# Layer A's output projection: where the transposed rows of the first two output units are read, and where the second unit is transposed

## The chip, the cores and the metric

The kernel runs on one core of a Trainium2 chip. The metric is the device time of one execution in microseconds (us). Engines are named as the profile names them: PE multiplies matrices, PEld loads its weights, DVE and ACT are the two engines for elementwise work, POOL here mostly issues small transfers, and SP issues the large ones. Each engine works through its own queue in order; semaphores join the queues.

## The reference: what is computed

Two layers act on a sequence of 256 rows and 2048 columns in f32. Layer A projects the normalised input to q, k, v and a gate, runs a chunked attention, multiplies by the gate and projects back from 4096 to 2048 columns, plus the residual. Layer B does the same with shared keys and values and a forget gate. What concerns the change is the last line of layer A and the first ones of layer B:

```python
x = x + (o * jax.nn.silu(g)) @ a_w_out[layer]
...
h_kv = rms_norm(x, kv_norm)
k_s, v_s = jnp.split(h_kv @ kv_w, 2, axis=-1)
...
h = rms_norm(x, b_norm[lb])
q, g = jnp.split(h @ b_w_in[lb], 2, axis=-1)
```

## The kernel before, in words

**Split operands.** An f32 product is made of three matmuls. Each operand is split into a rounded part `hi` (written by ACT) and the remainder `lo` (written by DVE from the raw value and `hi`); the products hi·hi, lo·hi and hi·lo are summed. Weights come in blocks of 128 x 1024 values (512 KB), loaded by SP into one of six `raw` buffers (`RAW = 6`, tag "raw"), split into one of four pairs of `hi` and `lo` buffers (`SPLIT = 4`), and consumed by PE. So a split can start only when PE is done with the split four places earlier, and a load only when the split that read the buffer is done.

**Feed.** `Feed` holds the whole list of weight blocks. `get` hands PE the next split pair; ahead of that, `fill` keeps four pairs (`DEPTH = 3` and the one handed out) prepared, and `refill` issues loads. `Feed.behind(dst, n)` writes a few elements of `dst` with an ACT instruction that reads the `hi` of the n-th prepared pair: later writers of `dst` then stand behind that split on ACT.

**Layer A's output projection** (`project`, with `ao_order`) makes four units `ao0` to `ao3` of 512 columns each. An entry of the order is a sub-block: a normal one (12 matmuls, one weight block of one unit) or a quad (`Quad.step`: 21 matmuls that do one block of each of two units, from four splits `quad_hi0` to `quad_hi3` of the two raw blocks and of differences of them; the two raw blocks are `one` and `two`). The second half of the order is four normal sub-blocks of `ao2` (its blocks 5 to 8), then quad 0, three normal ones (`ao2` blocks 9 to 11), quad 1, three normal ones, and so on to quad 4, with six normal sub-blocks of `ao3` at the end. In `Quad.split`, `t[:, :, 1]` (line 289) needs only the raw block `two`, `t[:, :, 0]` (line 288) both.

**Turned rows.** When a unit closes (`ao_closed`), its residual sum `xin` is complete (line 760). Layer B needs it transposed, as `x1T`, split again in hi and lo. For units 0 to 2 this is `x1_to_T`: `turn` transposes within 32 x 32 squares on DVE (line 487, into the one buffer `xinY`), 16 small transfers issued by POOL move the squares (line 490, into the one buffer `xinZ`), and four generator steps then read `xinZ`, each with two ACT copies (`x1Th`, line 150) and two DVE subtractions (`x1Tl`, line 151). The list that `ao_closed` returns, `[8, 1, 1, 1]`, says after how many further sub-blocks each of the four reading steps is issued. Unit 3 goes another way (`x_to_T`). The transposition of unit 1 writes the `xinY` that unit 0's 16 transfers read, and unit 1's transfers write the `xinZ` that unit 0's reading steps read.

**Loads of the residual.** `load_xin` (line 744) puts the input's columns of a unit on SP's queue, among the weight loads. The buffer `xin3` reuses storage that the transposition of `xin1` reads.

The order of instructions on each engine is set by the order of issue in this code and by a scheduler that may move an instruction ahead of others that do not depend on it.

Of the kernel before, what the change touches and what calls it, by code (L numbers as in the profile page):

```python
# [12 lines left out]
AF = mybir.ActivationFunctionType  # L13
# [3 lines left out]
P = 128  # L17
S = 256
NT = S // P
# [20 lines left out]
SQ = 32  # L40
# [25 lines left out]
def r32(ap):  # L66
    return ap.bitcast(F32)
# [8 lines left out]
def trunk(ctx, tc, x, x_t, gains, a_w_in, a_rel, a_w_out, kv_w, f_w, f_b, b_w_in, b_w_out, final_norm, out):  # L76
    nc = tc.nc
    pe, act, dve, pool, sp = nc.tensor, nc.scalar, nc.vector, nc.gpsimd, nc.sync
# [13 lines left out]
    def big_tile(shape, dt, name):  # L92
        return big.tile(shape, dt, name=name, tag="big")
# [54 lines left out]
    def split_x1(src, k, like=lambda v: v):  # L148
        hi, lo = like(x1T.h(k)), like(x1T.l(k))
        act.activation(hi, src, AF.Copy)  # L150
        dve.tensor_sub(lo, src, r32(hi))
# [10 lines left out]
    def x_to_T(src, k0):  # L162

        banks = []
        for c in range(0, 4, 2):
            ps = bank(f"xT_{k0 + c}")
            for i in range(2):
                for t in range(NT):
                    pe.transpose(ps[:, i * S + t * P:i * S + (t + 1) * P],
                                 src[t][:, (c + i) * P:(c + i + 1) * P], ident)  # L170
            banks.append(ps)
        for c in range(4):
            split_x1(banks[c // 2][:, c % 2 * S:(c % 2 + 1) * S], k0 + c)
            yield
# [13 lines left out]
    class Feed:  # L188
# [31 lines left out]
        def prepare(self, ahead=True, parts=(slice(None),)):  # L220
            if not self.loaded:
                self.begin()
            if not self.loaded:
                return
            spec, b, raw, (before, behind) = self.loaded.pop(0)
            if not spec:
                self.ready.append(b[0].split(b[1]))
                self.refill()
                return
            if before:  # L230
                before()
            nm, h = spec["name"], b - (spec["nk"] // KB - spec["late"])
            if 0 <= h < spec["kept"]:
                both = big_tile([P, 2, IL, KB, HN], F32R, f"{nm}_keep{b}")
                hi, lo = both[:, 0], both[:, 1]
            else:
                hi = stream.tile([P, IL, KB, HN], F32R, name=f"{nm}_hi{b}", tag="hi", bufs=SPLIT)
                lo = stream.tile([P, IL, KB, HN], F32R, name=f"{nm}_lo{b}", tag="lo", bufs=SPLIT)
            if spec["g0"] is not None:
                for j in range(KB):  # L240
                    gk = gain[:, spec["g0"] + b * KB + j:][:, :1]
                    act.activation(hi[:, :, j], raw[:, :, j], AF.Copy, scale=gk)  # L242
                    dve.scalar_tensor_tensor(lo[:, :, j], raw[:, :, j], gk, r32(hi[:, :, j]),  # L243
                                             op0=OP.mult, op1=OP.subtract)
                parts = ()
            for j in parts:
                act.activation(hi[:, :, j], raw[:, :, j], AF.Copy)  # L247
                dve.tensor_sub(lo[:, :, j], raw[:, :, j], r32(hi[:, :, j]))  # L248
            if behind:
                behind()  # L250
            self.ready.append((hi, lo))
            if ahead:
                self.refill()
# [8 lines left out]
        def behind(self, dst, n):  # L262

            act.activation(dst, r32(self.ready[n][0][:, :, 0, :1]), AF.Copy)
# [12 lines left out]
    class Quad:  # L277
# [4 lines left out]
        def split(self, i):  # L282

            one, two = self.raw
            t = self.all.t[:, 0]
            if not i:
                feed.behind(t[:, :, 0, :1], -1)
                dve.tensor_sub(t[:, :, 0], two[:, :, 0], one[:, :, 0])
                dve.tensor_sub(t[:, :, 1], two[:, :, 1], two[:, :, 0])
            src = [one, t, two[:, :, 1:], one][i]  # L290
            n = src.shape[2]
            hi = stream.tile([P, IL, KB, HN], F32R, name=f"quad_hi{i}", tag="hi", bufs=SPLIT)
            lo = stream.tile([P, IL, KB, HN], F32R, name=f"quad_lo{i}", tag="lo", bufs=SPLIT)
            act.activation(hi[:, :, :n], src, AF.Copy)
            dve.tensor_sub(lo[:, :, :n], src, r32(hi[:, :, :n]))  # L295
            if not i:
                dve.tensor_sub(one[:, :, 0], two[:, :, 1], t[:, :, 0])
                dve.tensor_sub(one[:, :, 1], one[:, :, 1], one[:, :, 0])
            return hi, lo
# [113 lines left out]
    feed = Feed(todo)  # L413
# [68 lines left out]
    def turn(src, n, name, queues=(pool,) * NQ, home=None):  # L482

        y, z = home or [att.tile([P, NQ, n, SQ], F32, name=name + i, tag=i) for i in "YZ"]
        dve.transpose(y, src.rearrange("p n (j u) -> p j n u", u=SQ))  # L487
        for i in range(NQ):
            for j in range(NQ):
                queues[j].dma_start(out=r32(z)[j * SQ:(j + 1) * SQ, i],  # L490
                                    in_=y[i * SQ:(i + 1) * SQ, j])
        return r32(z)
# [28 lines left out]
    def attention(g, biases, qk, vg, half, ocat, queues=(pool,) * NQ, line=(None, None), home=None):  # L521
# [44 lines left out]
        gT = z[:, :, HG * NB:].rearrange("p i (t h) u -> p h t i u", t=NT)  # L566
        yield
        ph, pl = split([pT[:, i, :NT] for i in range(HG)], "wide", line[1])
        yield
        op = bank("op").rearrange("p (i s) -> p i s", i=HG)  # L570
# [156 lines left out]
    x1T = Stat("x1T", KD)  # L727

    def x1_to_T(xin, u):
        z = turn(xin.rearrange("p t (c d) -> p (t c) d", d=P), NT * 4, "xin")  # L730
        xinT = z.rearrange("p i (t c) u -> p c t i u", t=NT)
        yield
        for i in range(4):
            feed.behind(x1T.h(u * 4 + i)[:, ::P][:, :, None], 2)
            for t in range(NT):
                split_x1(xinT[:, i, t], u * 4 + i,
                         lambda v: v[:, t * P:(t + 1) * P].rearrange("p (i u) -> p i u", u=SQ))
            yield

    xins, last = {}, []  # L740
# [5 lines left out]
    def add_combined(quads, u):  # L746
        dve.tensor_add(xins[u], xins[u], quads.comb[:, u % 2 * NT:u % 2 * NT + NT])
# [7 lines left out]
    def ao_closed(u, acc):  # L755
        if u % 2 == 0:
            add_combined(ao_quads, u)
        cs, xin = slice(u * UN, (u + 1) * UN), xins.pop(u)
        for t in range(NT):
            dve.tensor_add(xin[:, t], acc[t], xin[:, t])  # L760
            sp.dma_start(out=x1d[:, t, cs], in_=xin[:, t])
        more = None
        if u < 3:
            more = x1_to_T(xin, u)
            next(more)
        else:
            last.append(x_to_T([xin[:, t] for t in range(NT)], u * 4))
        for t in range(NT):
            act.activation(att.tile([P, UN], F32, name="junk", tag="tb"), xin[:, t], AF.Square,
                           accum_out=ssq1[:, t, u:u + 1])  # L770
        return more and (more, [8, 1, 1, 1])

    project(oA, ao, ao_order, ao_begun, ao_closed, [(prev, [2, 6, 2, 1]), (ao_quads.open(oA, QUADS), [3, 1, 1, 2, 2])])
    tot1 = const.tile([P, NT], F32, name="tot1")
    dve.tensor_reduce(tot1, ssq1, axis=AX.X, op=OP.add)
# [212 lines left out]
```

## Time and profile before

| | |
|---|---|
| time, median of 3 runs (lowest to highest) | 1761.28 us (1760.0 to 1762.1) |
| the profiled execution's own time | 1763.77 us |
| its span | 1762.0 us |
| DVE busy | 1244.3 us (71%) |
| ACT busy | 1109.4 us (63%) |
| POOL busy | 519.5 us (29%) |
| mean traffic of the DMA engines | 225 GB/s |

The time is that of a whole execution, the span that from the first to the last instruction in the trace. A row of an engine's timeline gives the start, the duration, the engine, the line, the operation with what it writes and reads, how many instructions were merged, and in brackets the idle time of the engine just before, with what ended it.

### The profile page before, as it was taken

The numbers are of one execution on the slowest core, as the hardware profiler recorded it, in microseconds if no ns is written. First come the engines' busy times: TensorE is split into PE (matmuls) and PEld (weight loads), VectorE is DVE, ScalarE is ACT, GpSimd is POOL, SyncE is SP. The second block draws the span as 40 slices with busy tenths as digits, with TensorE's granted clock in tenths as the row PEclk, the third lists the DMA queues.
The fourth block names the chain that finished last, engine by engine and source line by source line (L and its number), as shares of the span: only waits on it lengthen the run. The fifth ranks groups of instructions, "written<-read, shape, count | busy, mean of one in ns | idle before, by whom it ended". The sixth has DMA issues, their size and how long they took to land.

```text
span 1762.0 us, 25649 instructions
## 1 busy us (share of the span) xinstructions
PE 1741.4 (99%) x8348; PEld 1527.5 (87%) x8348; DVE 1244.3 (71%) x1818; ACT 1109.4 (63%) x2115; POOL 519.5 (29%) x1071
## 2 busy tenths in 40 slices
PE   9999999999999999998999999999999999999997
PEld 7888888888888888887888888888888888888886
DVE  7666666666666686687876777777777777876687
ACT  6555555555555566555656777777777777765454
POOL 1333333333333333212014333333333333333000
PEclk9999999999999999999999999999999999999999
DMA  8766767667677777676766777777777777777654
GB/s 299 241 223 221 226 224 223 223 225 225 224 226 228 224 224 234 196 246 208 241 218 217 238 226 226 226 226 227 226 225 224 225 225 226 229 229 239 218 201 145
DMA packets 143654, 396.35 MB, mean 225 GB/s; under 512 B 31104, under 2 KB 38560, under 8 KB 143392
## 3 DMA queue, kind: packets, MB, share of 16 engines
q1 hardware_dynamic: 107472, 354.25, 62.8%
q0 software_dynamic: 32256, 37.29, 6.5%
q10 hardware_dynamic: 3792, 3.17, 0.6%
q8 instruction: 66, 1.08, 0.2%
q14 instruction: 68, 0.56, 0.1%
HBM read 351.05 MB, written 4.23 MB: 202 GB/s over the span
## 4 chain that ended last, share of the span: by engine, by line
PE 92%; DMA 3%; DVE 2%; ACT 1%; issue 1%; POOL 1%; SPq 0%; DVEq 0%; POOLq 0%; ACTq 0%
PE bkv_acc L184 19%; PE bqg_acc L184 19%; PE aqk_acc L184 18%; PE avg_acc L184 18%; PE bo_acc L184 7%; PE ao_acc L184 4%; DMA sgZ<-sgY 1%; PE op L575 1%; PE s0p L541 1%; DMA xinZ<-xinY 1%; DVE quad_lo L295 1%; PE p L519 0%; PE p L518 0%; PE p L517 0%; PE op L518 0%
## 5 line engine op out<-in xcount | busy, mean ns | idle before, releaser
L490 POOL DMA_DIRECT2D sgZ<-sgY x512 | 251.7, 499 | 191.5 <-DVE sgY L487 112.5
L490 POOL DMA_DIRECT2D turned<-turned x448 | 220.7, 499 | 267.1 <-PE avg_acc L184 95.4
L243 DVE SCALAR_TENSOR_TENSOR bqg_lo<-bqg_raw,gain,bqg_hi 128x512 fp32r<-128x512 f32 x256 | 182.9, 752 | 83.6 <-ACT bqg_hi L242 83.3
L242 ACT ACTIVATE bqg_hi<-bqg_raw,gain 128x512 fp32r<-128x512 f32 x256 | 170.6, 714 | 104.4 <-PE bqg_acc L184 49.8
L248 DVE TENSOR_TENSOR avg_lo<-avg_raw,avg_hi 128x1024 fp32r<-128x1024 f32 x127 | 153.4, 1219 | 109.0 <-ACT avg_hi L247 107.3
L248 DVE TENSOR_TENSOR aqk_lo<-aqk_raw,aqk_hi 128x1024 fp32r<-128x1024 f32 x125 | 152.4, 1220 | 86.7 <-ACT aqk_hi L247 86.7
L243 DVE SCALAR_TENSOR_TENSOR bkv_lo<-bkv_raw,gain,bkv_hi 128x512 fp32r<-128x512 f32 x256 | 181.2, 748 | 40.9 <-ACT bkv_hi L242 38.1
L247 ACT ACTIVATE avg_hi<-avg_raw 128x1024 fp32r<-128x1024 f32 x127 | 132.5, 1056 | 120.8 <-PE aqk_acc L184 68.5
L184 PE MATMUL aqk_acc<-aqk_hi,xTh 128*128 128x512 f32 x512 | 191.1, 384 | 0.9 <-ACT aqk_hi L247 0.9
L184 PE MATMUL bqg_acc<-bqg_hi,x1Th 128*128 128x512 f32 x512 | 191.4, 384 | 0.0
L184 PE MATMUL avg_acc<-avg_hi,xTh 128*128 128x512 f32 x512 | 190.2, 382 | 0.0
L184 PE MATMUL aqk_acc<-aqk_lo,xTh 128*128 128x512 f32 x512 | 189.4, 380 | 0.7 <-DVE aqk_lo L248 0.7
L184 PE MATMUL aqk_acc<-aqk_hi,xTl 128*128 128x512 f32 x512 | 189.3, 380 | 0.0
L184 PE MATMUL bkv_acc<-bkv_hi,x1Th 128*128 128x512 f32 x512 | 189.0, 379 | 0.0
L247 ACT ACTIVATE aqk_hi<-aqk_raw 128x1024 fp32r<-128x1024 f32 x125 | 131.6, 1052 | 91.1 <-PE aqk_acc L184 43.5
L184 PE MATMUL bkv_acc<-bkv_hi,x1Tl 128*128 128x512 f32 x512 | 188.8, 379 | 0.0
L184 PE MATMUL avg_acc<-avg_hi,xTl 128*128 128x512 f32 x512 | 188.8, 379 | 0.0
L184 PE MATMUL bqg_acc<-bqg_hi,x1Tl 128*128 128x512 f32 x512 | 188.8, 379 | 0.0
L184 PE MATMUL bqg_acc<-bqg_lo,x1Th 128*128 128x512 f32 x512 | 188.8, 379 | 0.0
L184 PE MATMUL bkv_acc<-bkv_lo,x1Th 128*128 128x512 f32 x512 | 188.8, 379 | 0.0
L184 PE MATMUL avg_acc<-avg_lo,xTh 128*128 128x512 f32 x512 | 188.8, 379 | 0.0
L242 ACT ACTIVATE bkv_hi<-bkv_raw,gain 128x512 fp32r<-128x512 f32 x256 | 168.8, 712 | 25.5 <-PE bqg_acc L184 18.9
(300 smaller groups left out, 3562.6 us busy)
## 6 DMA issues: line engine op xcount, KB each, us to landing
bqg_raw<-in_b_w_in SPq DMA_DIRECT2D x128, 512.0 KB, 4.3
bkv_raw<-in_kv_w SPq DMA_DIRECT2D x128, 512.0 KB, 4.2
avg_raw<-in_a_w_in SPq DMA_DIRECT2D x127, 512.0 KB, 4.2
aqk_raw<-in_a_w_in SPq DMA_DIRECT2D x125, 512.0 KB, 4.1
ao_raw<-in_a_w_out SPq DMA_DIRECT2D x64, 512.0 KB, 4.3
bo_raw<-in_b_w_out SPq DMA_DIRECT2D x64, 512.0 KB, 4.2
sgZ<-sgY POOLq DMA_DIRECT2D x512, 40.0 KB, 4.0
turned<-turned POOLq DMA_DIRECT2D x448, 32.0 KB, 3.7
```

What stands on the lines that cost most here:

```text
L184: pe.matmul(acc[t], x[:, t * P:(t + 1) * P], w, start=t not in begun, stop=last and i == 2)
L242: act.activation(hi[:, :, j], raw[:, :, j], AF.Copy, scale=gk)
L243: dve.scalar_tensor_tensor(lo[:, :, j], raw[:, :, j], gk, r32(hi[:, :, j]), op0=OP.mult, op1=OP.subtract)
L247: act.activation(hi[:, :, j], raw[:, :, j], AF.Copy)
L248: dve.tensor_sub(lo[:, :, j], raw[:, :, j], r32(hi[:, :, j]))
L295: dve.tensor_sub(lo[:, :, :n], src, r32(hi[:, :, :n]))
L490: queues[j].dma_start(out=r32(z)[j * SQ:(j + 1) * SQ, i], in_=y[i * SQ:(i + 1) * SQ, j])
L541: pe.matmul(s0p[:, i], q0[:, i], qkT[:, HG + i, 0], start=True, stop=True)
L575: pe.matmul(op[:, i, P:], v1[:, i * DH:(i + 1) * DH], pT[:, i, NT], start=False, stop=i == HG - 1)
```

## The change

The four reading steps no longer use `behind`. Instead they are issued under `tc.issue_after(feed.by_act.ins)`: the ACT instructions in the block are put behind the last `hi` split given so far on ACT's queue, without a semaphore. For that, `prepare` and `Quad.split` keep the last `hi` and `lo` instruction. Units 0 and 2 have their reading steps start after 11 sub-blocks, not 8. Unit 1 is no longer transposed when it closes: its transposition is a step of its own, 8 sub-blocks later and behind the last given `lo` split on DVE, and its first reading step comes 7 sub-blocks after that.

```diff
             for j in parts:
-                act.activation(hi[:, :, j], raw[:, :, j], AF.Copy)
-                dve.tensor_sub(lo[:, :, j], raw[:, :, j], r32(hi[:, :, j]))
+                self.by_act = act.activation(hi[:, :, j], raw[:, :, j], AF.Copy)
+                self.by_dve = dve.tensor_sub(lo[:, :, j], raw[:, :, j], r32(hi[:, :, j]))
...
-            act.activation(hi[:, :, :n], src, AF.Copy)
-            dve.tensor_sub(lo[:, :, :n], src, r32(hi[:, :, :n]))
+            feed.by_act = act.activation(hi[:, :, :n], src, AF.Copy)
+            feed.by_dve = dve.tensor_sub(lo[:, :, :n], src, r32(hi[:, :, :n]))
...
     def x1_to_T(xin, u):
-        z = turn(xin.rearrange("p t (c d) -> p (t c) d", d=P), NT * 4, "xin")
+        if u % 2:
+            yield
+            with tc.issue_after(feed.by_dve.ins):
+                z = turn(xin.rearrange("p t (c d) -> p (t c) d", d=P), NT * 4, "xin")
+        else:
+            z = turn(xin.rearrange("p t (c d) -> p (t c) d", d=P), NT * 4, "xin")
         xinT = z.rearrange("p i (t c) u -> p c t i u", t=NT)
         yield
         for i in range(4):
-            feed.behind(x1T.h(u * 4 + i)[:, ::P][:, :, None], 2)
-            for t in range(NT):
-                split_x1(xinT[:, i, t], u * 4 + i,
-                         lambda v: v[:, t * P:(t + 1) * P].rearrange("p (i u) -> p i u", u=SQ))
+            with tc.issue_after(feed.by_act.ins):
+                for t in range(NT):
+                    split_x1(xinT[:, i, t], u * 4 + i,
+                             lambda v: v[:, t * P:(t + 1) * P].rearrange("p (i u) -> p i u", u=SQ))
             yield
...
-        return more and (more, [8, 1, 1, 1])
+        return more and (more, [8, 7, 1, 1, 1] if u % 2 else [11, 1, 1, 1])
```

What this does to the queues is shown at three places. Names such as `ao2_hi8` are block 8 of unit 2; `quad_hi0` to `quad_hi3` right behind it are the four splits of quad 0. Line numbers are those of the kernel that is listed.

ACT around quad 0, before: the first reading step (`x1Th0<-xinZ`, unit 0) stands directly behind the first of the four splits.

```order
L247 ACTIVATE ao2_hi8_7549<-ao2_raw8_7413 128x1024
L769 ACTIVATE junk_7543,ssq1_6777<-xin1_7447 128x512
L264 ACTIVATE x1Th0_6778<-ao2_hi8_7549 128x2
L264 ACTIVATE ao_quad_6864<-ao2_hi8_7549 128x2
L769 ACTIVATE junk_7545,ssq1_6777<-xin1_7447 128x512
L294 ACTIVATE quad_hi0_7577<-ao2_raw0_7431 128x1024
L150 ACTIVATE x1Th0_6778<-xinZ_7369 128x128 x2
L264 ACTIVATE x1Th0_6778<-quad_hi0_7577 128x2
L150 ACTIVATE x1Th0_6778<-xinZ_7369 128x128 x2
L294 ACTIVATE quad_hi1_7600<-ao_quad_6864 128x1024
```

The same place with the change:

```order
L247 ACTIVATE ao2_hi8_7530<-ao2_raw8_7413 128x1024
L774 ACTIVATE junk_7524,ssq1_6777<-xin1_7447 128x512
L264 ACTIVATE ao_quad_6864<-ao2_hi8_7530 128x2
L774 ACTIVATE junk_7526,ssq1_6777<-xin1_7447 128x512
L294 ACTIVATE quad_hi0_7553<-ao2_raw0_7431 128x1024
L294 ACTIVATE quad_hi1_7571<-ao_quad_6864 128x1024
L294 ACTIVATE quad_hi2_7587<-ao3_raw0_7433 128x2x256
L150 ACTIVATE x1Th0_6778<-xinZ_7369 128x128 x2
L294 ACTIVATE quad_hi3_7613<-ao2_raw0_7431 128x1024
L247 ACTIVATE ao2_hi9_7625<-ao2_raw9_7469 128x1024
```

The first reading step now has three of quad 0's splits ahead of it, and `quad_hi3` behind it; the small `behind` writes of `x1Th0` are gone.

DVE at the same place, before, with the second unit's transposition (`xinY_7524<-xin1`):

```order
L248 TENSOR_TENSOR ao2_lo8_7550<-ao2_raw8_7413,ao2_hi8_7549 128x1024
L288 TENSOR_TENSOR ao_quad_6864<-ao3_raw0_7433,ao2_raw0_7431 128x2x256
L487 STREAM_TRANSPOSE xinY_7524<-xin1_7447 128x1024
L151 TENSOR_TENSOR x1Tl0_6780<-xinZ_7369,x1Th0_6778 128x128 x2
L295 TENSOR_TENSOR quad_lo0_7578<-ao2_raw0_7431,quad_hi0_7577 128x1024
L151 TENSOR_TENSOR x1Tl0_6780<-xinZ_7369,x1Th0_6778 128x128
L297 TENSOR_TENSOR ao2_raw0_7431<-ao3_raw0_7433,ao_quad_6864 128x2x256
```

DVE with the change:

```order
L248 TENSOR_TENSOR ao2_lo8_7531<-ao2_raw8_7413,ao2_hi8_7530 128x1024
L288 TENSOR_TENSOR ao_quad_6864<-ao3_raw0_7433,ao2_raw0_7431 128x2x256
L295 TENSOR_TENSOR quad_lo0_7554<-ao2_raw0_7431,quad_hi0_7553 128x1024
L297 TENSOR_TENSOR ao2_raw0_7431<-ao3_raw0_7433,ao_quad_6864 128x2x256
L298 TENSOR_TENSOR ao2_raw0_7431<-ao2_raw0_7431 128x2x256
L295 TENSOR_TENSOR quad_lo1_7572<-ao_quad_6864,quad_hi1_7571 128x1024
L295 TENSOR_TENSOR quad_lo2_7588<-ao3_raw0_7433,quad_hi2_7587 128x2x256
L151 TENSOR_TENSOR x1Tl0_6780<-xinZ_7369,x1Th0_6778 128x128 x2
L295 TENSOR_TENSOR quad_lo3_7614<-ao2_raw0_7431,quad_hi3_7613 128x1024
L289 TENSOR_TENSOR ao_quad_6864<-ao3_raw1_7536 128x2x256
L248 TENSOR_TENSOR ao2_lo9_7626<-ao2_raw9_7469,ao2_hi9_7625 128x1024
```

The transposition has left this place; three `quad_lo` stand ahead of the first `x1Tl`. Line 289 of the next quad still stands ahead of `ao2_lo9`. The transposition is now among quad 1's splits on DVE:

```order
L151 TENSOR_TENSOR x1Tl0_6780<-xinZ_7369,x1Th0_6778 128x128 x2
L295 TENSOR_TENSOR quad_lo2_7710<-ao3_raw1_7536,quad_hi2_7709 128x2x256
L487 STREAM_TRANSPOSE xinY_7725<-xin1_7447 128x1024
L295 TENSOR_TENSOR quad_lo3_7745<-ao2_raw1_7534,quad_hi3_7744 128x1024
L248 TENSOR_TENSOR ao2_lo12_7757<-ao2_raw12_7617,ao2_hi12_7756 128x1024
L289 TENSOR_TENSOR ao_quad_6864<-ao3_raw2_7652 128x2x256
```

The last row there is line 289 of quad 2, behind `ao2_lo12`.

SP's queue, before; `ao2_raw1` and `ao3_raw1` are the blocks `one` and `two` of quad 1, `xin3` the last residual:

```order
L206 DMA ao2_raw1_7553<-in_a_w_out 128x1024
L744 DMA xin3_8184<-in_x 128x2x512
L206 DMA ao3_raw1_7555<-in_a_w_out 128x1024
L206 DMA ao2_raw12_7652<-in_a_w_out 128x1024
L206 DMA ao2_raw13_7664<-in_a_w_out 128x1024
```

SP's queue with the change:

```order
L206 DMA ao2_raw1_7534<-in_a_w_out 128x1024
L206 DMA ao3_raw1_7536<-in_a_w_out 128x1024
L206 DMA ao2_raw12_7617<-in_a_w_out 128x1024
L206 DMA ao2_raw13_7629<-in_a_w_out 128x1024
L206 DMA ao2_raw14_7641<-in_a_w_out 128x1024
L206 DMA ao2_raw2_7650<-in_a_w_out 128x1024
L206 DMA ao3_raw2_7652<-in_a_w_out 128x1024
L749 DMA xin3_8176<-in_x 128x2x512
L206 DMA ao3_raw5_7748<-in_a_w_out 128x1024
```

The load of `xin3` has moved behind six weight loads. POOL's queue keeps its order: 16 transfers of unit 0, 16 of unit 1, 16 of unit 2. On PE no instruction moves against another.

## The prediction

> **What bounds the kernel now.** I read the page's first part, then the list of PE's waits over the whole span, then the table of stretches around the output projection.
>
> ```profile
> PE 1741.4 (99%) x8348; PEld 1527.5 (87%) x8348; DVE 1244.3 (71%) x1818; ACT 1109.4 (63%) x2115; POOL 519.5 (29%) x1071
> ...
> PE p L518 <- DVE quad_lo L295: 2.9, 2, 1.7
> PE ao_acc L184 <- DVE ao_lo L248: 2.2, 1, 2.2
> PE op L517 <- ACT wideh L509: 2.0, 2, 1.7
> ...
> PE ao_acc L518 <- DVE quad_lo L295: 0.3, 1, 0.3
> ...
> 780.00:803.30 23.30, 23.30 (x109) 20.41 (x108) 15.87 (x18) 10.84 (x21) 7.90 (x16) 1.00 0.81 282
> 803.30:819.00 15.70, 10.28 (x36) 7.42 (x35) 13.76 (x22) 8.93 (x17) 6.59 (x14) 0.89 0.63 190
> 819.00:880.00 61.00, 61.00 (x284) 53.41 (x284) 52.25 (x66) 37.97 (x60) 3.84 (x9) 1.00 0.67 224
> ```
>
> The first row says that PE is the bound: only PE's gaps can be won. The waits (total, times, longest) show one cluster, `p` and `ao_acc` on `quad_lo` and `ao_lo`: 2.9 + 2.2 + 0.3 = 5.4 us. In the stretches (length, then busy time of PE, PEld, DVE, ACT and POOL, granted clock, DMA share, GB/s) PE is full before 803.3 and after 819.0; between them it is busy 10.28 of 15.70 us, and the granted clock is 0.89. That is quad 0. PE's timeline gives the loss exactly:
>
> ```profile
> 803.31 0.38 PE L517 MATMUL p<-quad_hi,oAh 128*128 128x512 f32 x1
> 805.42 0.48 PE L518 MATMUL p<-quad_lo,oAh 128*128 128x512 f32 x1 [1.73 <-DVE quad_lo L295]
> ...
> 814.44 0.48 PE L184 MATMUL ao_acc<-ao_lo,oAh 128*128 128x512 f32 x1 [2.17 <-DVE ao_lo L248]
> ...
> 814.98 0.38 PE L184 MATMUL ao_acc<-ao_hi,oAh 128*128 128x512 f32 x1
> 815.87 0.63 PE L184 MATMUL ao_acc<-ao_hi,oAh 128*128 128x512 f32 x1
> 818.43 0.55 PE L184 MATMUL ao_acc<-ao_hi,oAh 128*128 128x512 f32 x1
> 818.82 0.38 PE L184 MATMUL ao_acc<-ao_lo,oAh 128*128 128x512 f32 x1
> 823.79 0.38 PE L517 MATMUL p<-quad_hi,oAh 128*128 128x512 f32 x1
> 836.09 0.38 PE L517 MATMUL p<-quad_hi,oAh 128*128 128x512 f32 x1
> ```
>
> The first, and the last two, are the first matmuls of quads 0, 1 and 2. A quad and three normal sub-blocks are 21 + 36 = 57 matmuls: quad 1 to quad 2 takes 12.30 us (0.2158 us a matmul), quad 0 to quad 1 takes 20.48. **The loss is 8.18 us.** Idle time is 5.4 of it; in the stretch behind, six matmuls from 815.87 to 818.43 take 0.427 us each. The rest is restarts.
>
> Why do the splits come late? The queues around it:
>
> ```profile
> 795.75 1.06 ACT L294 ACTIVATE quad_hi<-ao_raw 128x1024 fp32r<-128x1024 f32 x1
> 802.59 0.51 ACT L150 ACTIVATE x1Th<-xinZ 128x128 fp32r<-128x128 f32 x2 [5.79 <-DMA xinZ<-xinY]
> ...
> 802.61 1.25 DVE L487 STREAM_TRANSPOSE xinY<-xin 128x1024 f32<-128x1024 f32 x1 [6.54 <-DMA xinZ<-xinY]
> ...
> 804.15 1.22 DVE L295 TENSOR_TENSOR quad_lo<-ao_raw,quad_hi 128x1024 fp32r<-128x1024 f32 x1
> ...
> 808.43 0.68 DVE L295 TENSOR_TENSOR quad_lo<-ao_raw,quad_hi 128x512 fp32r<-128x512 f32 x1
> ...
> 812.56 0.69 DVE L289 TENSOR_TENSOR ao_quad<-ao_raw 128x512 f32<-128x512 f32 x1 [1.91 <-DMA ao_raw<-in_a_w_out]
> 813.17 3.49 DVE L248 TENSOR_TENSOR ao_lo<-ao_raw,ao_hi 128x1024 fp32r<-128x1024 f32 x3
> ...
> 803.93 0.38 SPq L744 DMA_DIRECT2D xin<-in_x  x1
> 809.14 0.33 SPq L206 DMA_DIRECT2D ao_raw<-in_a_w_out  x1
> ```
>
> One event holds three queues: unit 0's 16 transfers land at 802.5. ACT has `quad_hi0` done at 796.8 and then sits 5.79 us at the first reading step, which needs `xinZ`. DVE sits 6.54 us at unit 1's transposition, which overwrites the `xinY` still being sent, although `quad_hi0` is ready for it. SP sits until the transposition has read `xin1` and `xin3` can load; behind that stands quad 1's block `two`, which finally starts at 809.14, when `quad_lo2` (808.43 + 0.68) frees its buffer. It lands at 812.5, line 289 waits 1.91 us for it, and `ao_lo9`, next on DVE, is PE's last wait.
>
> **The change part by part.** PE reaches quad 0 at 803.31 either way, since nothing ahead of 795 us changes but a `behind` write. From there I set the new queues against PE's need (estimates from these rows). Splits are paced by PE, as this row shows:
>
> ```profile
> 793.15 1.06 ACT L247 ACTIVATE ao_hi<-ao_raw 128x1024 fp32r<-128x1024 f32 x1 [1.53 <-PE ao_acc L184]
> ```
>
> A `hi` starts when PE finishes the sub-block four splits earlier; normal ones take 12 x 0.2158 = 2.59 us, so the four ahead of quad 0 end at 795.54, 798.13, 800.72 and 803.31.
>
> *Unit 0's first read, moved behind `quad_hi2`.* ACT: `quad_hi0` 795.75, `quad_hi1` 798.2 to 799.3, `quad_hi2` 800.8 to 801.4, then the wait for 802.5 (1.1 us where it was 5.79), two copies to 803.1, `quad_hi3` 803.5 to 804.6. DVE: `quad_lo0`, lines 297 and 298 by 799.3, `quad_lo1` to 800.5, `quad_lo2` to 802.1, two `x1Tl` to 803.5, `quad_lo3` 804.7 to 805.9. PE wants `quad_lo3` after 15 matmuls and one more: 803.31 + 3.45 = 806.77. Spare: 0.9 us; as ACT then waits for PE and not for the landing, the landing could slip from 802.5 to about 803.9 before PE notices. The three waits on `quad_lo` (1.73 is the longest) go. What is late next is `ao_lo9`.
>
> *Unit 1's transposition and the load of `xin3` off this place.* Block `two` of quad 1 is now next on SP and starts when `quad_lo2` is done, 802.1. Its landing is the one term not shown: bounds are in the first row below, minimum, median and maximum of these loads' time to landing.
>
> ```profile
> DMA to landing us min/median/max: 3.1/4.4/7.6
> ...
> 795.00:800.00 5.00, 5.00 (x25) 4.38 (x24) 1.07 (x2) 1.69 (x4) 1.49 (x3) 1.00 1.02 370
> 800.00:805.00 5.00, 3.69 (x18) 2.89 (x16) 2.39 (x4) 2.31 (x8) 0.00 (x0) 1.00 0.13 49
> ```
>
> The DMA engines are full (1.02) up to 800 and nearly empty (0.13) from then, so I take the time of the load that started at 809.14 into as empty a machine, 812.5 - 809.1 = 3.4 us: landed at 805.5. Line 289 then follows `quad_lo3` without a wait, 805.9 to 806.5, and `ao_lo9` ends at 807.7. PE needs it after 22 matmuls, 808.06. Spare: 0.4 us. With 4.4 us it would end at 808.3 (cost 0.2), with 7.6 at 811.5 (cost 3.4).
>
> *The transposition at its new place,* among quad 1's splits, and the other reads of unit 0 there. DVE's work from `quad_lo3` to `ao_lo12` by the rows: eight 128 x 1024 `lo` at 1.16 (3.49 / 3), one half `lo` and lines 289, 288, 297 and 298 at 0.6, six `x1Tl` at 0.2, the transposition 1.2: 14.7 us, from 804.7 to 819.4. PE, started at quad 1 at 803.31 + 12.30 = 815.61, wants `ao_lo12` after 22 matmuls, 820.36. The queue is nearly solid but 1 us ahead, and quad 1's `quad_lo3`, one `lo` earlier, is ready at 818.2 for a need at 815.61 + 3.45 = 819.06. I cost it at nothing; without that cover it is the transposition's 1.2 us.
>
> *Unit 1's transfers and reads.* They start near 817. How long such 16 take, from the first issue to the first read:
>
> ```profile
> 787.58 3.94 POOL L490 DMA_DIRECT2D xinZ<-xinY  x8 [48.87 <-DVE xinY L487]
> 809.81 4.90 POOL L490 DMA_DIRECT2D xinZ<-xinY  x10 [10.84 <-DVE x1Tl L151]
> ...
> 823.28 0.51 ACT L150 ACTIVATE x1Th<-xinZ 128x128 fp32r<-128x128 f32 x2 [1.02 <-DMA xinZ<-xinY]
> 890.24 1.71 ACT L150 ACTIVATE x1Th<-xinZ 128x128 fp32r<-128x128 f32 x8 [5.13 <-DMA xinZ<-xinY]
> ```
>
> 14.9 us for unit 0 (to 802.5), 13.5 for unit 1. So they land by 832. The read stands behind quad 3's `quad_hi1`, which PE's pace puts at 840.2 - 5.2 = 835.0: 3 us spare, no wait. `xin3` is loaded behind the transposition near 817 and used when unit 3 closes, far off; SP's next load behind it waits for `quad_lo3` anyway.
>
> *Unit 2, and the removed writes.* Unit 2's reads are issued at the projection's end as before, in the same places; its landing, 890.2 in the last row above, moves earlier together with PE, which did not wait for it before. Twelve `behind` writes go, each under 0.2 us of an ACT that is not the bound: nothing.
>
> **Sum.** 1763.77 (this execution) - 8.18 + 0 = 1755.59 us. This execution lies 2.49 us above the median of the runs, 1761.28; from the median the same sum is **1753.1 us**.
>
> The slow matmuls are 1.7 us of the 8.18: ten from 814.98 to 818.82 take 3.84 us where 2.16 are due. The trace has them only right behind the idle pieces; the stretches on both sides have a clock of 1.00. [...]
>
> **Rivals.**
>
> *The block `two` of quad 1 lands late (10%).* A load into traffic takes up to 7.6 us, and line 289 stands ahead of `ao_lo9` in the new order too. Against it speaks the share of 0.13. At the maximum 3.4 us return: 1756.5.
>
> *The slow stretch has a cause of its own (6%).* [...] 1753.1 + 1.7 = 1754.8.
>
> *The loss moves to quad 1 (6%).* If DVE, nearly solid from 804.7, falls behind with the transposition, quad 1's last splits and line 289 of quad 2 come late as here; a full repeat gives all 8.2 us back: no change, 1761. Against it: about 1 us spare at each point. That the change does not do what it says ends here too, but the queues show that it does.
>
> *Slower (4%).* ACT takes its queue in order, and the first read still has `quad_hi3` and all later splits behind it. Beyond 803.9 every us of a later landing costs PE one us. It decides against the change only past 803.9 + 8.2 + 3.5 = 815.6, twice the 14.9 us that unit 0's transfers took; a landing at 817 gives 1766.
>
> The forecast, no new wait over a few tenths, has 74%.
>
> **Range and chances.** The forecast's own spread is about 2 us, the runs' own and a median for a median; the late block reaches 1756.5. From 1751.0 to 1757.5 holds these and the slow stretch, and leaves out the last two rivals and small tails. Faster by over 0.2% (3.5 us, about what a measurement of this kernel can tell from no change) means under 1757.8: forecast and the first two rivals, 0.90. Within 0.2%: 0.06. Slower: 0.04.
>
> **What would show it.** In the profile after: PE's waits without `quad_lo` and `ao_lo` of the output projection; quad 0 to quad 1 in 12.3 us; ACT's idle at the first `x1Th` about 1 us; no idle on DVE ahead of the transposition, which now stands behind quad 1's third `lo`; SP's load of `two` starting near 802; a clock of 1.00 throughout. An idle piece on PE ahead of `ao_lo9` with a DMA wait at line 289 would show the first rival, a wait on quad 1's splits the third.

## The result, and the profile after

The changed kernel takes 1754.49 us (median of six runs, 1752.58 to 1757.04), the kernel before 1761.03 (six runs, 1759.31 to 1762.12). The ratio is 0.9962, with a 95% interval of 0.9952 to 0.9972: 6.5 us less, where 8.2 were forecast. The profiled execution took 1757.04 us, with a span of 1755.3.

PE's waits over the whole span of the changed kernel (total, times, longest), those of the output projection:

```profile
PE ao_acc L184 <- DVE ao_lo L248: 0.5, 1, 0.5
```

The three rows on `quad_lo` and `ao_lo` with 5.4 us are gone; one wait of 0.5 us on an `ao_lo` is there instead. The stretches around it:

```profile
803.30:819.00 15.70, 15.70 (x75) 13.75 (x74) 14.61 (x20) 10.97 (x17) 1.83 (x4) 1.00 0.63 209
819.00:880.00 61.00, 60.54 (x280) 52.50 (x279) 52.86 (x70) 36.14 (x56) 14.82 (x31) 1.00 0.79 255
```

PE is now busy through all of the first one, at a clock of 1.00; in the second it has lost 0.46 us. PE's timeline, the first matmuls of quads 0 to 4, with the wait between the third and the fourth:

```profile
802.98 0.38 PE L517 MATMUL p<-quad_hi,oAh 128*128 128x512 f32 x1
815.28 0.38 PE L517 MATMUL p<-quad_hi,oAh 128*128 128x512 f32 x1
827.58 0.38 PE L517 MATMUL p<-quad_hi,oAh 128*128 128x512 f32 x1
832.96 0.48 PE L184 MATMUL ao_acc<-ao_lo,oAh 128*128 128x512 f32 x1 [0.46 <-DVE ao_lo L248]
840.62 0.38 PE L517 MATMUL p<-quad_hi,oAh 128*128 128x512 f32 x1
853.10 0.38 PE L517 MATMUL p<-quad_hi,oAh 128*128 128x512 f32 x1
```

Quad 0 to quad 1 takes 12.30 us, as forecast, and so does the next step; the last two take 13.04 and 12.48. The queues at the places that were held before (ACT, DVE, SP):

```profile
800.59 0.63 ACT L294 ACTIVATE quad_hi<-ao_raw 128x512 fp32r<-128x512 f32 x1 [1.53 <-PE ao_acc L184]
801.54 0.51 ACT L150 ACTIVATE x1Th<-xinZ 128x128 fp32r<-128x128 f32 x2 [0.33 <-DMA xinZ<-xinY]
803.18 1.06 ACT L294 ACTIVATE quad_hi<-ao_raw 128x1024 fp32r<-128x1024 f32 x1 [1.12 <-PE ao_acc L184]
...
805.49 0.69 DVE L289 TENSOR_TENSOR ao_quad<-ao_raw 128x512 f32<-128x512 f32 x1
815.40 1.23 DVE L487 STREAM_TRANSPOSE xinY<-xin 128x1024 f32<-128x1024 f32 x1
...
801.97 7.97 SPq L206 DMA_DIRECT2D ao_raw<-in_a_w_out  x5
```

ACT waits 0.33 us for unit 0's transfers instead of 5.79, and then for PE. DVE reaches the transposition at 815.40 without idling, and line 289 without a wait for its load, because SP starts block `two` of quad 1 at 801.97, 7.2 us sooner. The one wait of PE left stands behind the same line as the old fourth one, two quads later. DVE's timeline there:

```profile
831.07 0.69 DVE L289 TENSOR_TENSOR ao_quad<-ao_raw 128x512 f32<-128x512 f32 x1 [0.98 <-DMA ao_raw<-in_a_w_out]
831.68 3.49 DVE L248 TENSOR_TENSOR ao_lo<-ao_raw,ao_hi 128x1024 fp32r<-128x1024 f32 x3
```

Line 289 waits 0.98 us for a weight block, and the `ao_lo` queued behind it is late. The load of that block was not held on SP this time; it took longer to land, 4.2 us where block `two` of quad 1 took 3.4 (the last experiment).

### The profile page after: what moved, and what is told of

Read it like the earlier page. It is cut to its first block, busy times and chain, and to the rows that moved or that the text cites. A ratio compares the mean times of both kernels' runs of the same rounds, so it can differ in the third digit from the quotient of the medians.

```text
span 1755.3 us, 25640 instructions
## 1 busy us (share of the span) xinstructions
PE 1738.7 (99%) x8348; PEld 1527.7 (87%) x8348; DVE 1243.2 (71%) x1818; ACT 1107.2 (63%) x2103; POOL 516.6 (29%) x1071
## 4 chain that ended last, share of the span: by engine, by line
PE 96%; DMA 1%; DVE 1%; ACT 0%; issue 0%; SPq 0%; POOL 0%; DVEq 0%; ACTq 0%
PE bkv_acc L184 19%; PE bqg_acc L184 19%; PE avg_acc L184 18%; PE aqk_acc L184 18%; PE bo_acc L184 8%; PE ao_acc L184 7%; PE op L575 1%; PE s0p L541 1%; PE p L519 0%; PE p L517 0%; PE p L518 0%; PE op L518 0%; PE s1p L518 0%; PE s1p L519 0%; PE s1p L517 0%; PE op L519 0%
```

## The experiments

In what follows a step is the time from one quad's first matmul to the next one's; 12.30 us is a step without loss. "The stage" is the time from quad 0's first matmul to the first one of layer B.

**More profiles of both kernels.** Nothing is edited. The changed kernel twice more:

> The changed kernel as it is, a second profile and five more rounds. Theory A (what is left of the forecast 8.2 us is one small new wait, 0.46 us on an ao_lo split behind line 289, and by chance a slow stretch of PE's clock at 1540 us that the first profile of this kernel had and the one of before had not): the wait on ao_lo near 832 us comes back at 0 to 1 us, the slow stretch at 1540 us need not, and the ratio comes out between 0.9945 and 0.9970. Theory B (the change itself brings the slow stretch at 1540 us): it is there again, 1.7 us long, and the ratio is not under 0.9955.

> The changed kernel once more, beside the next one on the same chip. Theory A: quad 0 to quad 1 in 12.3 us; a wait of 0 to 1 us on an ao_lo split at quad 2; ratio 0.995 to 0.9975. A slow stretch of PE's clock, if any, behind the wait at 1540 us.

and the kernel before twice more:

> The kernel before as it is, for a second profile. Theory A: the idle pieces at quad 0 come back at 4.5 to 6.5 us, quad 0 to quad 1 takes 18.5 to 21 us; the slow stretches of PE's clock, one behind the idle pieces at 815 us in the first profile, none at 1547 us behind a wait of 1.74 us, are not the same ones again if the clock only follows chance after a wait. Theory B (the idle pieces at quad 0 always cost a slow stretch): it is there again, 3 to 4 us long, at 815 us.

> The kernel before, a third profile. Theory A (the slow stretch behind quad 0's waits is chance): from quad 0 to layer B's first matmul 76.0 to 77.8 us, with a slow stretch at the upper end and without one at the lower; the waits at quad 0 are 4.5 to 6.5 us either way.

The changed kernel came out at ratios of 0.9967 (0.9957 to 0.9978) and 0.9963 (0.9951 to 0.9975), the kernel before against itself at 1.0002 (0.9992 to 1.0011). The steps from the profiles:

| profile | step 0 to 1 | 1 to 2 | 2 to 3 | 3 to 4 | the stage |
|---|---|---|---|---|---|
| before, first | 20.48 | 12.30 | 12.30 | 12.31 | 77.46 |
| before, second | 18.24 | 13.38 | 12.30 | 12.30 | 76.30 |
| before, third | 18.20 | 13.14 | 12.30 | 12.30 | 76.01 |
| changed, first | 12.30 | 12.30 | 13.04 | 12.48 | 70.19 |
| changed, second | 12.30 | 12.30 | 13.13 | 12.63 | 70.43 |
| changed, third | 12.30 | 12.30 | 12.60 | 12.64 | 69.92 |

Read it by rows: the kernel before loses 8.18, 7.02 and 6.74 us over its steps (mean 7.3), the changed one 0.92, 1.16 and 0.64 (mean 0.9). The means of the stage, 76.59 and 70.18, differ by 6.4 us, and the times by 6.5: the change acts in this stage and nowhere else that could be seen. The second profile of the kernel before, at the idle pieces:

```profile
813.13 0.48 PE L184 MATMUL ao_acc<-ao_lo,oAh 128*128 128x512 f32 x1 [2.13 <-DVE ao_lo L248]
...
812.00:818.00 6.00, 4.87 (x23) 4.28 (x24) 5.97 (x7) 1.06 (x1) 3.45 (x8) 1.00 0.86 283
```

It has the same wait on `ao_lo9`, 2.13 us, but the granted clock behind it is 1.00, where the first profile had a slow stretch (0.66 from 814 to 819 us). The slow stretch was no fixed part of the loss; with it absent, the step of 18.24 us came out a little under the 18.5 named.

The kernel before has an extra 0.8 to 1.1 us at the second step in the two profiles without the slow stretch, and none in the one with it. In the second profile PE waits 0.36 us on a `quad_lo` and 0.17 us on an `ao_lo` of quad 1. One reading, not tested: PE, not slowed, reaches quad 1 sooner than DVE has caught up, so that the slow stretch had hidden part of a lateness that was there anyway.

**Only the transposition late.**

```diff
-        return more and (more, [8, 7, 1, 1, 1] if u % 2 else [11, 1, 1, 1])
+        return more and (more, [8, 7, 1, 1, 1] if u % 2 else [8, 1, 1, 1])
```

> Only unit 1's transposition is late (8, then 7 sub-blocks); unit 0's reads start after 8 as before. Theory A (ACT, held at unit 0's first read until its transfers land at about 802, is one block, DVE at the transposition another, and each costs by itself): ACT still idles 4 to 6 us ahead of the first x1Th; PE waits once on quad_lo, about 1 to 2 us, and about 2 us on ao_lo9 because block two of quad 1 starts near 807 us instead of 802; quad 0 to quad 1 takes 16 to 18.5 us (12.3 with the whole change, 20.5 before); the time is 2 to 5 us under before. Rival (the transposition on DVE was the only block): quad 0 to quad 1 takes 12.3 to 13.5 us and the time is that of the whole change.

Ratio 0.9991 (0.9981 to 1.0001); step 0 to 1 takes 18.06 us. Its ACT and DVE:

```profile
801.77 0.91 ACT L150 ACTIVATE x1Th<-xinZ 128x128 fp32r<-128x128 f32 x4 [5.42 <-DMA xinZ<-xinY]
802.59 1.04 ACT L294 ACTIVATE quad_hi<-ao_quad 128x1024 fp32r<-128x1024 f32 x1
...
809.69 0.69 DVE L289 TENSOR_TENSOR ao_quad<-ao_raw 128x512 f32<-128x512 f32 x1 [1.79 <-DMA ao_raw<-in_a_w_out]
```

ACT is held 5.42 us ahead of the second split, so the third is late, block `two` starts late (SP at 806.38) and line 289 waits for it. The mechanism is as expected; the gain is 1.6 us by the ratio, under the 2 to 5 us named, with an interval that reaches from nothing to 3.3. This profile has a slow stretch behind the wait on `ao_lo9` (granted clock 0.66 from 811 to 816 us).

**Only the reads late.**

```diff
-        if u % 2:
-            yield
-            with tc.issue_after(feed.by_dve.ins):
-                z = turn(xin.rearrange("p t (c d) -> p (t c) d", d=P), NT * 4, "xin")
-        else:
-            z = turn(xin.rearrange("p t (c d) -> p (t c) d", d=P), NT * 4, "xin")
+        z = turn(xin.rearrange("p t (c d) -> p (t c) d", d=P), NT * 4, "xin")
...
-        return more and (more, [8, 7, 1, 1, 1] if u % 2 else [11, 1, 1, 1])
+        return more and (more, [8, 1, 1, 1] if u % 2 else [11, 1, 1, 1])
```

> Only unit 0's reads are late (after 11 sub-blocks, units 0 and 2); unit 1 is transposed when it closes, as before. Theory A: DVE idles about 6 us ahead of the transposition until 802, quad_lo0 starts near 804 us; PE waits two or three times on quad_lo, 2.5 to 4 us together; line 289 now stands behind ao_lo9 in the scheduler's order, so ao_lo9 costs nothing; quad 0 to quad 1 takes 15.5 to 18.5 us; the time is 2.5 to 5.5 us under before. Rival (the first read on ACT was the only block): 12.3 to 13.5 us and the time of the whole change. The two gains do not add up to the whole, if either part alone leaves a block standing.

Ratio 0.9996 (0.9986 to 1.0005): nothing gained, where 2.5 to 5.5 us were expected. Its DVE, ACT and PE:

```profile
801.94 1.25 DVE L487 STREAM_TRANSPOSE xinY<-xin 128x1024 f32<-128x1024 f32 x1 [5.92 <-DMA xinZ<-xinY]
...
832.27 1.71 ACT L150 ACTIVATE x1Th<-xinZ 128x128 fp32r<-128x128 f32 x8 [4.11 <-DMA xinZ<-xinY]
...
834.55 0.48 PE L517 MATMUL ao_acc<-quad_hi,ao_sums 128*128 128x512 f32 x1 [1.40 <-ACT quad_hi L294]
```

Quad 0 behaves as expected (DVE held 5.92 us, step 0 to 1 14.86, a little under the range). But unit 1's reads, issued by the same counts as before, were moved by the scheduler into one lump of eight ahead of quad 2's third split; ACT waits 4.11 us there for unit 1's transfers, and step 2 to 3 takes 16.46 us, part of it a slow stretch (granted clock 0.72 from 834 to 840 us). What was gained at quad 0 was lost at quad 2. So neither of these two kernels brings a gain over the whole time that can be told from none, and the whole change brings 6.5 us. But this one does not show what late reads of unit 0 alone are worth, since it also put unit 1's reads in a new place; at quad 0 they did shorten the step, to 14.86 us from 18.20 to 20.48.

**The counts without the ties.**

```diff
-            with tc.issue_after(feed.by_dve.ins):
+            if True:
...
-            with tc.issue_after(feed.by_act.ins):
-                for t in range(NT):
...
+            for t in range(NT):
...
```

> The whole change without the two ties (issue_after): the same counts of sub-blocks, but nothing keeps the reads behind given splits. The scheduler then puts all eight copies of unit 0 behind quad_hi0 and the transposition ahead of quad_lo0 again. Theory A (the place in the queues is what counts, not the number in the list): the idle pieces at quad 0 come back, quad 0 to quad 1 takes 19 to 22 us, the time is within 3 us of before; unit 1's reads, now ahead of quad 1's third split, may add a wait of 0 to 3 us at quad 1. Rival (the counts alone do it): the time of the whole change.

Ratio 1.0015 (1.0005 to 1.0025), slower than before. Its ACT:

```profile
801.31 1.71 ACT L150 ACTIVATE x1Th<-xinZ 128x128 fp32r<-128x128 f32 x8 [4.72 <-DMA xinZ<-xinY]
802.92 1.04 ACT L294 ACTIVATE quad_hi<-ao_quad 128x1024 fp32r<-128x1024 f32 x1
...
822.00 1.31 ACT L150 ACTIVATE x1Th<-xinZ 128x128 fp32r<-128x128 f32 x6 [3.40 <-DMA xinZ<-xinY]
```

Step 0 to 1 takes 19.41 us, with a slow stretch (granted clock 0.72 from 812 to 818 us), and step 1 to 2 14.82. The number in the list only says when the instruction is issued; without a tie the scheduler moved it ahead to the old place, and unit 1's reads to a worse one.

**The old kind of tie with the new counts.**

```diff
         for i in range(4):
-            with tc.issue_after(feed.by_act.ins):
...
+            feed.behind(x1T.h(u * 4 + i)[:, ::P][:, :, None], 2)
...
```

> The whole change, but the reads are tied with the small behind writes on ACT as before, not with issue_after. Theory A (only the place matters; the writes of under 0.2 us each hide under ACT's idle time): same queues, quad 0 to quad 1 in 12.3 us, the time within 1.5 us of the whole change. Rival (the removed writes are part of the gain): 1.5 us or more above it.

Ratio 0.9956 (0.9942 to 0.9970), the steps 12.30, 12.30, 12.30 and 12.48, the stage 69.45 us: as good as the change. The removed writes were no part of the gain; which tie is used for the reads does not matter here (the transposition kept its tie on DVE).

**The first read one sub-block sooner.**

```diff
-        return more and (more, [8, 7, 1, 1, 1] if u % 2 else [11, 1, 1, 1])
+        return more and (more, [8, 7, 1, 1, 1] if u % 2 else [10, 1, 1, 1])
```

> The whole change with unit 0's reads after 10 sub-blocks, not 11: the first read stands behind quad_hi1, ahead of quad_hi2. Theory A (block two of quad 1 cannot start before quad_lo2, lands 3.4 us later, and line 289 ahead of ao_lo9 waits for it): no wait on quad_lo, but a wait on ao_lo9 of 0.5 to 2.5 us, with a DMA wait of 1 to 3 us at line 289 near 805 us; time 0.5 to 3 us over the whole change. Rival (one place earlier costs nothing, since the transfers land at about 801.5 and PE needs quad_lo2 only at 805): no wait, the time of the whole change.

Its DVE and PE:

```profile
802.28 0.69 DVE L295 TENSOR_TENSOR quad_lo<-ao_raw,quad_hi 128x512 fp32r<-128x512 f32 x1 [0.23 <-ACT quad_hi L294]
806.40 0.69 DVE L289 TENSOR_TENSOR ao_quad<-ao_raw 128x512 f32<-128x512 f32 x1 [1.55 <-DMA ao_raw<-in_a_w_out]
...
808.28 0.48 PE L184 MATMUL ao_acc<-ao_lo,oAh 128*128 128x512 f32 x1 [1.58 <-DVE ao_lo L248]
```

In this profile the place counts: with the read ahead of the third split, block `two` starts only when `quad_lo2` ends at 802.97, against a PE that began quad 0 at 801.79 in this profile; it lands 3.4 us later, and PE waits 1.58 us on `ao_lo9`, with no wait on `quad_lo`. The stage takes 72.18 us, 2.0 over the changed kernel's mean. The time (ratio 0.9967, 0.9956 to 0.9978) does not tell the two apart.

**The load of `xin3` late.**

```diff
-                sp.dma_start(out=raw[:, :, j], in_=spec["w"][b][:, :, j])
+                self.by_sp = sp.dma_start(out=raw[:, :, j], in_=spec["w"][b][:, :, j])
...
-        if left == 4:
-            load_xin(xf, u)
+        if left == (9 if u == 3 else 4):
+            with tc.issue_after(feed.by_sp.ins) if u == 3 else ExitStack():
+                load_xin(xf, u)
```

> The whole change, and the load of xin3 (512 KB) put some 14 weight loads later on SP. Theory A (the new wait of 0.46 us near 832 us comes from traffic: xin3 and unit 1's 16 transfers on top of the weights delay block two of quad 3 or 2, line 289 waits 0.98 us for it, and ao_lo is late): line 289's DMA wait there shrinks to under 0.4 us and PE's wait on ao_lo to under 0.1; the time is 0 to 1.5 us under the whole change. Rival (the 16 transfers alone do it, or a block starts late because its buffer is freed late): the wait stays at 0.3 us or more.

> The whole change with the load of xin3 late, once more. Theory A (the new wait near 832 us comes from xin3's traffic on top of unit 1's 16 transfers): again all four steps from quad to quad take 12.3 us, and from quad 0 to layer B's first matmul it takes 0.8 to 1.3 us less than in the changed kernel; the time 0 to 1.5 us less, which the interval may not tell. Rival (its absence in the first such run was chance, as the changed kernel without issue_after had none either): a wait of 0.3 us or more at quad 2 or 3.

The DMA row by stretch, 815 to 831 us, of the changed kernel's first profile:

```profile
815.00:831.00 16.00, 16.00 (x76) 14.03 (x75) 12.88 (x14) 9.65 (x11) 7.85 (x16) 1.00 0.83 263
```

and of the late load's first one, with its line 289:

```profile
815.00:831.00 16.00, 16.00 (x76) 13.99 (x75) 13.76 (x15) 10.13 (x12) 7.84 (x16) 1.00 0.74 238
...
829.37 0.69 DVE L289 TENSOR_TENSOR ao_quad<-ao_raw 128x512 f32<-128x512 f32 x1
```

The DMA engines are busy 0.74 of the stretch (0.70 in the second profile) instead of 0.83, at least in part because the 512 KB of `xin3` are no longer in it. Line 289 waits 0 (0.25) instead of 0.98 us, and PE does not wait there. The steps are 12.30, 12.30, 12.31, 12.30 and 12.30, 12.31, 12.31, 12.56; the stage 69.28 and 69.55, 0.8 us under the changed kernel's mean. The ratios are 0.9958 (0.9942 to 0.9974) and 0.9952 (0.9939 to 0.9964), the second beside the changed kernel's 0.9963 on the same chip: in the right direction, with intervals that overlap. That this kernel is the faster one is seen in the stage of both profiles and not shown for the time.

Whether block `two` of quad 3 starts late or lands late can be read from the traces. Its start is given in us ahead of quad 2's first matmul:

| profile | block started | landed after | wait of line 289 | last five of unit 1's transfers issued from | DMA share, 826.5 to 830 |
|---|---|---|---|---|---|
| changed, first | 0.74 | 4.2 | 0.98 | 826.98 | 0.99 |
| changed, second | 0.73 | 4.3 | 1.07 | 826.47 | 0.93 |
| changed, third | 0.74 | 3.8 | 0.54 | 826.41 | 0.94 |
| old kind of tie | 0.80 | 3.5 | 0.23 | 826.58 | 0.92 |
| late load, first | 0.74 | 3.2 | 0 | 823.57 | 0.48 |
| late load, second | 0.57 | 3.3 | 0.25 | 825.40 | 0.65 |

The block does not start later in the changed kernel; it lands later. The early `xin3` itself is out of the way by then: in the first profile its load starts at 816.66 and lands 6.0 us later, before the block starts at 826.84. What meets the block are the last of unit 1's 16 transfers, which come sooner when `xin3` is loaded late. That this is the whole cause is not shown: the kernel with the old kind of tie loads `xin3` early, has as many transfers and nearly the share there, and no wait of PE at that step in its one profile. And the small loss at the last step (0.18 to 0.34 us in the changed kernel) is there with the late load too, 0.26 us in its second profile.

## Why the prediction was right, and which term was off

The forecast time of 1753.1 us and the measured 1754.49 differ by 1.4, within the range; the forecast gain was 1.6 us too large. Two terms were off, both in the same direction, so no error hid another. Point by point:

- **One late landing holds three queues**: right. With ACT alone freed, DVE still idles 5.92 us; with DVE alone freed, ACT still idles 5.42 us, and SP starts block `two` at 806.38 instead of 801.97.
- **Unit 0's read behind `quad_hi2`, spare on `quad_lo3`**: right. ACT then waits 1.12 us for PE, not PE for ACT.
- **Block `two` started near 802 and line 289 without a wait**: right (801.97, and no idle at 805.49). With the read one sub-block sooner the spare is gone and the wait is on `ao_lo9`, the place named.
- **The transposition at quad 1 at no cost**: right at quad 1, step 12.30.
- **No new wait anywhere**: wrong by 0.9 us. The sum looked at the DMA engines only around 800. The last of unit 1's transfers were on them together with block `two` of quad 3 at 826.5 to 830; the first rival's mechanism, a block that lands late ahead of line 289 (4.2 us after its start, at a share of 0.99, in the first profile), appeared at quad 2, a place that the prediction had passed over.
- **The loss of 8.18 us**: mis-sized. The three profiles of the kernel before lose 8.18, 7.02 and 6.74. The slow stretch of 1.7 us is in the first alone; the others lose 0.8 to 1.1 at the second step instead. Taking one execution's loss for that of every execution made the term about 0.9 us too large. That the 1.7 us would go with the waits was the author's estimate; no run shows what lowers the clock.
- **A clock of 1.00 throughout**: right in this stage, in all three profiles of the changed kernel; not elsewhere (0.74 behind a wait in layer B, in the last section).

7.3 - 0.9 = 6.4 us, against 6.5 measured. The rival that the slow stretch has a cause of its own and would stay was not what happened: it is gone from this stage in all three profiles of the changed kernel. That alone proves little, since two of the three profiles of the kernel before have none either. Over all profiles here it comes (granted clock 0.66 to 0.72) in four of the six in which PE waits 1.8 us or more in all at one quad (the kernel before and the first three edits), right behind such waits, and in none of the other seven. So it went with the waits, and not in every execution. That block `two` of quad 1 did not land late and that the loss did not move to quad 1 follows from the first two steps of 12.30 us; the time itself rules out the rival of a slower kernel.

## What to carry to other kernels

Here an instruction that waited for a far-off transfer held everything queued behind it, on its own engine (ACT 5.79 us, DVE 6.54 us) and, through buffers and loads, on others (SP started block `two` at 809.14 us, and at 801.97 with the change). Put such an instruction behind the last work that does not need it, tie it there (the scheduler undid the mere count here, and step 0 to 1 took 19.41 us), and look at every queue that the same event holds: the two kernels here that freed one of two gained nothing over the whole time that could be measured, one of them because other reads were moved to a worse place. And size a loss from several profiles: one had 20% more than the other two.

## What the runs showed of the hardware

PE's clock after waits of 1.4 to 2.5 us was not the same from one execution to the next of one kernel. In the changed kernel's first profile, the wait on `op` in layer B, and what follows:

```profile
1538.58 0.39 PE L517 MATMUL op<-wideh,vh 128*128 128x256 f32 x1 [1.36 <-ACT wideh L509]
...
1540.77 0.63 PE L184 MATMUL bqg_acc<-bqg_lo,x1Th 128*128 128x512 f32 x1
1542.91 0.63 PE L184 MATMUL bqg_acc<-bqg_hi,x1Th 128*128 128x512 f32 x1
...
1538.50:1545.00 6.50, 6.34 (x24) 5.21 (x25) 5.16 (x10) 4.34 (x10) 4.19 (x9) 0.74 0.60 171
```

The same place in its second profile:

```profile
1539.47 0.38 PE L517 MATMUL op<-wideh,vh 128*128 128x256 f32 x1 [1.93 <-ACT wideh L509]
...
1538.00:1545.00 7.00, 5.46 (x28) 4.72 (x29) 5.39 (x11) 5.52 (x11) 4.54 (x10) 1.00 0.64 198
```

A wait of 1.36 us was followed by a mean clock of 0.74, with five matmuls from 1540.77 to 1542.91 at 0.43 us each; one of 1.93 us was not, with 1.00. In the third profile a wait of 2.52 us was, with 0.62 from 1541 to 1545. Behind the waits at quad 0 of the kernel before, the clock was lower in one profile of three, 0.66 from 814 to 819 us, and 1.00 in the other two. What decides in the single case was not tried.
